# Weight parts kept in DRAM and an order from other durations, in the input projection of a decoder layer

## The chip, the cores and the metric

The kernel runs on one core of one Trainium2 chip. The metric is the device time of one execution in microseconds. The core's engines are TensorE (PE, matmuls; PEld is its weight loads), VectorE (DVE), ScalarE (ACT), GpSimd (POOL) and SyncE (SP), whose queue issues nearly all DMAs here.

## The reference

One layer of a hybrid decoder in float32, 2048 tokens of width 1024. Each half of the layer is normalised before and after. The first half projects the tokens once, splits the result into an mLSTM group and an attention group (MLA), and projects both back. The second half is an MLP.

```python
a   = rmsnorm(x, norm_pre_mix)
proj = a @ w_in                   # 1024 -> 1960 columns, 16 units of 128 in the kernel
qk_ml = silu(causal_conv(qk_ml, conv_w, conv_b))       # q, k of 4 mLSTM heads
h_ml = mlstm_chunkwise(q_ml, k_ml, v_ml, i_gate, f_gate)
h_ml = rmsnorm(h_ml) * sigmoid(o_ml)
q  = rmsnorm(c_q, q_norm) @ w_uq                       # c_q: 256 columns of proj
kv = rmsnorm(c_kv, kv_norm) @ w_ukv                    # c_kv: 128 columns
k_rope = apply_rope(k_r, cos, sin)
h_mla = causal_block_attention(q, k, v)                # 8 heads
x = x + rmsnorm(concat(h_ml, h_mla) @ w_out)
x = x + rmsnorm(square(relu(rmsnorm(x) @ w_up)) @ w_down)
```

## The kernel before, in words

Every float32 matmul is made of three matmuls in a faster 32-bit format (`mm3`, lines 198 to 200): each operand is split into a rounded part `h` (a cast) and the remainder `l` (a subtract), and h·h, h·l and l·h are summed. So every operand costs a cast and a subtract on other engines.

The input projection takes the tokens in four blocks of 512 (b = 0 to 3). Per block there are 16 units of 128 output columns; the units 13, 14, 15 are the latents of attention, 0 the gates and rotary keys, 1 to 4 the convolved q and k, 5 to 8 the values (whose four weights are used together), 9 to 12 the output gates. `ORDER` gives their sequence. For every block the weights of every unit are loaded anew from the input (`wu`, 512 KB), cast by ACT (line 376) and subtracted by DVE, or by Pool for the units in `WPOOL` (line 381). The raw tiles share four buffers (`awr`) with raw token tiles, the parts have four buffers each (`wh`, `wl`).

Behind a unit's matmuls come its own steps. For the latents (`latents_in`): multiply by the token scale (`norm` in block 0, `evac` later), square on ACT (line 537), sum over the partitions by TensorE with a column of ones (`sums_`, line 543, results in `ssp`), statistics, loads of the scale, gain and split. For the gates (`stabiliser`): transposes to token rows (`gates`), a polynomial of many small DVE steps (`g1` to `g3`), transposes back (`g4`, line 693, result `rp`), then scans. `chunk` is the mLSTM recurrence over 128 tokens, spread between the matmuls of values and gates.

Nothing of this order is left to chance. A planner (`Plan`) simulates all operations of the whole kernel with a duration for each (the number in `pl.op("DVE", 602, ...)`), buffer rings, and a key for priority; the sequence that it finds is pinned on TensorE, ACT, DVE and Pool, and DMA issues are emitted in it. On the chip each engine runs its instructions in that order and waits when one is not ready. Attention, the output projection and the MLP follow in the same plan; their first steps overlap with the last chunk.

Of the kernel before, what the change touches and what calls it, by code (L numbers as in the profile page):

```python
# [18 lines left out]
P = 128  # L19
# [29 lines left out]
QLO = 1  # L49
TLATE = 5.0  # L50
LEAD = 20.0
VLEAD = 3.0
# [4 lines left out]
XLEAD = 10.0  # L57
WLEAD = 18.0
SPLIT = 5.0
# [6 lines left out]
WPOOL = (1, 2, 3, 4)  # L66
LGAIN = 20.0
CPOOL = True
KPOOL = (0, 1, 2)
VPOS = (2, 2, 2, 4)  # L70
KROT = 50.0
XB = 4
FIN = (4, 6)
FK = 1.0
PINNED = ("PE", "Activation", "DVE", "Pool")
# [114 lines left out]
def trunk(ctx: ExitStack, tc: tile.TileContext, x, xT, pos, wu, uqw, ukw, uvw, wout, wup, wdn, cols, rows, consts, edge, out, dbg=None):  # L190
# [66 lines left out]
    for name, bufs in (  # L257
        ("awr", WR), ("wh", 4), ("wl", 4), ("mm", 2), ("pst", 1), ("cc", 1), ("cbc", 1), ("G", 1), ("raw", 2), ("cy", 2), ("cth", 2),
        ("rsbc", 2), ("tg", 1), ("R", 1), ("aS", 2), ("E", 2), ("iwbc", 1), ("qs", 1), ("num", 1), ("kv", 1), ("kw", 1), ("hn", HN), ("ho", HO),
        *((f"x{x}{k}", 2 if k < XDB else 1) for k in range(KD) for x in "hl"),  # L260
    ):
        pl.ring(name, bufs)
# [61 lines left out]
    def xsplit(b):  # L324
        def pair(j):
# [35 lines left out]

    def wsplit(b, u):
        t = {}
# [34 lines left out]
        t["free"] = [("wh", first[0][0]), ("wl", first[0][1])]  # L398
        return t

    unit_ops = []

    def unit(b, u):
        w = wsplit(b, u)
# [9 lines left out]
        for k in range(KD):  # L414
            last = pl.op(
                "PE", 648, lambda k=k: mm(k), [w["op"][k], *o_x[b, k]] + ([last] if k else []), kA(b, TIME[b][u]), take=() if k else ("mm",),
                free=w["free"] + x_holders[b, k],
            )
            if k == 0:
                t["head"] = last  # L420
            unit_ops.append(last)
# [3 lines left out]
    def statistics(nm, n, sums, o_sums, mul, add, key):  # L425
# [23 lines left out]
        o = pl.op("DVE", 75, ms, o_sums, key)  # L449
        t["op"] = o = pl.op("Pool", 300 + 165 * n, rs, [o, o_fill], key)  # L450
        if nm == "x0":
            return t
        h = pl.op("PE", 110, tr, [o, o_cst], key, take=("pst",))
        o = pl.op("DVE", 202, put, [h], key, free=[("pst", h)])
# [5 lines left out]
    def xstats(b):  # L460
# [27 lines left out]
        if b == 0:  # L488
            o_fill3.extend(pl.op("Pool", 1776, lambda i=i: fills3(i), ends if i else [x for k in range(4, KD) for x in o_x[0, k]], key=kA(0, 20)) for i in range(2))
# [19 lines left out]
        else:  # L509
            h = pl.op("PE", 860, spread, [t["op"], o_cst], key, take=("pst",))  # L510
            o_rsbc[b] = pl.op("Activation", 478, put, [h], key, take=("rsbc",), free=[("pst", h)])

    def latents_in(b):
# [4 lines left out]
        def one(i):  # L518
# [19 lines left out]

            def sums_():
                if i == 0:  # L540
# [5 lines left out]
            if b == 0:  # L546
                o = pl.op("Activation", 478, evac, [u["op"], *t.get("o", [])], key, take=take, free=[("mm", u["head"])])
                head = o
                o = pl.op("DVE", 602, norm, [o, o_rsbc[b]], key, free=[("rsbc", o_rsbc[b])])
            else:  # L550
                o = pl.op("DVE", 602, evac, [u["op"], o_rsbc[b], *t.get("o", [])], key, take=take, free=[("mm", u["head"]), ("rsbc", o_rsbc[b])])
# [3 lines left out]
            s = pl.op("Activation", 520, sq, [o], key, take=("cth",))  # L555
            o = pl.op("PE", 750, sums_, [s, o_fill, *sums], key, take=() if i else ("pst",), free=[("cth", s)])
# [6 lines left out]
        def total():  # L563
            ssc = e2.tile([P, 12], F32, tag="ssc", name=f"ssc{b}")
            vec.tensor_copy(ssc, t["p"][:, 0:12])
            ss8 = t["ss8"] = e2.tile([P, 8], F32, tag="ss8", name=f"ss8{b}")
            vec.tensor_tensor(ss8[:, 0:4], ssc[:, 0:4], ssc[:, 4:8], ALU.add)
            vec.tensor_scalar(ss8[:, 0:4], ss8[:, 0:4], QSCALE2 / 256, QSCALE2 * EPS, ALU.mult, ALU.add)
            vec.tensor_scalar(ss8[:, 4:8], ssc[:, 8:12], 1.0 / 128, EPS, ALU.mult, ALU.add)

        o = pl.op("DVE", 546, total, sums, key, free=[("pst", sums[0])])
# [13 lines left out]
        def split(i):  # L585
# [9 lines left out]
            g = pl.op("DVE", 663, lambda: gain(i), [l, o], late, free=[("cbc", l)])  # L595
            h = pl.op("Activation", 520, hi, [g], late, take=("cth",))
            d = pl.op("Pool" if CPOOL else "DVE", 1225 if CPOOL else 602, lo, [h], late)
# [11 lines left out]
    def rotate(b, t, G):  # L609
# [8 lines left out]

        eng, cost = (pool, ("Pool", 1225)) if b in KPOOL else (vec, ("DVE", 602))

# [15 lines left out]
        g = pl.op("SP", 500, load, o_rope, key, take=("tg",), kb=128)  # L636
# [3 lines left out]
        h = pl.op("Activation", 520, hi, [o], key)  # L640
# [6 lines left out]
    def stabiliser(b):  # L647
# [5 lines left out]
        def evac():  # L653
            t["Gr"] = e2.tile([P, TB], F32R, tag="G", name=f"G{b}", bufs=1)
# [131 lines left out]
    def conv(b, j):  # L786
# [35 lines left out]
        r = pl.op("Pool", 160, head, [o_fill, *halos.get((b - 1, j), [])], key, take=("raw",))  # L822
        e = pl.op("DVE", 602, evac, [r, u["op"], o_rsbc[b]], key, free=[("mm", u["head"]), ("rsbc", o_rsbc[b])])
        halos[b, j] = [pl.op("Pool", 160, tail, [e], key, free=[("raw", r)])]
        y = o = pl.op("Activation", 707, tap0, [e], key, take=("cy",), free=[("raw", r)])
        for i in range(1, 4):
            o = pl.op("DVE", 663, lambda i=i: tap(i), [o], key, free=[("raw", r)])
        h = pl.op("Activation", 520, tanh, [o], key, take=("cth",))
        war = [x for c in range(4) for x in o_chunk.get((b - 2, c), {}).get("qk", [])]
        o_qk[b, j] = [  # L830
            pl.op("DVE", 602, lambda i=i: put(i), [h, *war, *(o_fill3 if j < 2 else [])], key, free=[("cy", y), ("cth", h)])
# [3 lines left out]
    def values(b):  # L835

        ws = [wsplit(b, 5 + i) for i in range(4)]

        def one(c):
# [13 lines left out]
            for k in range(KD):  # L853
                last = pl.op(
                    "PE", 648, lambda k=k: mm(k), [ws[k // 2]["op"][0], *o_x[b, k]] + ([last] if k else []), kA(b, TIME[b][5 + c]),
# [6 lines left out]
            o_vx[b, c] = pl.op("Activation", 571, evac, [last, rs_x[b]["op"], *war], kA(b, TIME[b][5 + c] + 2), free=[("mm", head)])  # L862
# [4 lines left out]
    def gates(b, h):  # L867
# [9 lines left out]
        o = pl.op("DVE", 602, lambda: vec.tensor_tensor(g, u["p"], rsbc[b], ALU.mult), [u["op"], o_rsbc[b], *war], key, free=[("mm", u["head"]), ("rsbc", o_rsbc[b])])  # L877
        o = pl.op("Activation", 520, lambda: act.activation(g, g, AF.Tanh, scale=0.5), [o], key)
        o_gate[b, h] = pl.op("DVE", 396, gain, [o], key)

    def chunk(b, c):
# [121 lines left out]
        o = pl.op("Activation", 1172, exps, [e, o_sc_in[b]], key)  # L1003
        o = pl.op("Pool", 594, causal, [o], key)
        w = pl.op("DVE", 602, weigh, [o, s], key, free=[("aS", s)])
        q = pl.op("Pool", 1400, scale_q, [i, *qk], key, take=("qs",), free=[("iwbc", i)])
# [3 lines left out]
        k = pl.op("PE", 220, turn_k, [*qk, o_cst], key, take=("kv",))  # L1010
        kw = pl.op("DVE", 340, weigh_k, [k, o_sc_in[b]], key, take=("kw",), free=[("kv", k)])
        out["state"], out["v"], out["qk"] = [], [n], [s, q, k]
        for p in range(2):
            m = pl.op("PE", 430, lambda p=p: update(p), [kw, o_vx[b, c]], key, take=("kv",), free=[("kw", kw)])
            out["state"].append(pl.op("DVE", 528, lambda p=p: state(p), [m, n], key, free=[("kv", m)]))
            out["v"].append(m)
        a = pl.op("DVE", 273, norm1, [n], key)
        o = pl.op("Activation", 1106, norm2, [a], key)
        o = pl.op("DVE", 564, norm3, [o], key)
        o = pl.op("Pool", 958, norm4, [o, o_fill], key)  # L1020
        hn = pl.op("DVE", 680, norm5, [o], key, take=("hn",), free=[("num", n)])
        gs = [o_gate[b, i] for i in range(4)]
        h = pl.op("PE", 440, turn_h, [hn, *gs], key, take=("aS",), free=[("hn", hn)])
        g = pl.op("DVE", 602, gated, [h], key, take=("ho",), free=[("aS", h)])
# [3 lines left out]
    def rope_tables():  # L1028
# [5 lines left out]
        o2 = pl.op("DVE", 70, lambda: vec.tensor_scalar(off2, off, 2 * math.pi, None, ALU.mult), [o_rest], key)  # L1034
# [1514 lines left out]
```

## Time and profile before

| | |
|---|---|
| Median of 3 runs | 2485.22 us (2483.44 to 2487.77) |
| Profiled execution, its own time | 2481.76 us |
| Its span, first to last instruction | 2480.1 us |
| Input projection in the span | about 0 to 480 us |
| TensorE busy | 97% of the span |
| DMA moved | 378.14 MB, mean 152 GB/s |

The busy share of TensorE counts matmuls that overlap in its pipeline, so the distance from one matmul's start to the next says more than one's length. A released wait is named by the instruction whose end released it.

### The profile page before, as it was taken

What the parts mean: (1) busy time and instruction counts of PE and PEld (TensorE: products, weight loads), DVE (VectorE), ACT (ScalarE), POOL (GpSimd) and SP (SyncE); (2) the same over time, 40 slices, a digit from 0 to 9 for tenths busy, and PEclk for the clock granted to TensorE, in tenths of its full rate; (3) what the DMA queues carried; (4) which work ended last, traced back from release to release, by engine and by line L of the source; (5) the groups of instructions that cost most, each with busy time, mean ns of one, the idle gap of its engine ahead of it and who ended that gap; (6) DMA issues with size and microseconds to landing.
All of it is one profiled execution on the core that took longest, in us unless ns stands there. A gap on an engine that the chain in (4) does not pass through costs nothing.

```text
span 2480.1 us, 34020 instructions
## 1 busy us (share of the span) xinstructions
PE 2409.3 (97%) x11091; PEld 1940.9 (78%) x11091; DVE 1808.1 (73%) x3214; ACT 1349.9 (54%) x2625; POOL 863.6 (35%) x728
## 2 busy tenths in 40 slices
PE   8999999999999999999999999999999999999997
PEld 6778787767777777688888888888888888888875
DVE  5867667588888878745866678776676687776688
ACT  5535443367777777644666657665674343443343
POOL 3442424358898898532100000000000333332235
PEclk9999999999999999999999999999999999999998
DMA  6554544510000000476777799656574445445556
GB/s 222 150 164 144 171 152 134 146 49 15 17 21 12 13 15 11 146 230 217 263 215 212 236 283 275 201 167 186 170 238 151 153 129 178 132 143 157 188 165 226
DMA packets 308026, 378.14 MB, mean 152 GB/s; under 512 B 32028, under 2 KB 218408, under 8 KB 307656
## 3 DMA queue, kind: packets, MB, share of 16 engines
q1 hardware_dynamic: 304264, 368.58, 48.7%
q0 software_dynamic: 3584, 7.39, 1.1%
q8 instruction: 87, 1.43, 0.2%
q14 instruction: 91, 0.75, 0.1%
HBM read 251.93 MB, written 121.85 MB: 151 GB/s over the span
## 4 chain that ended last, share of the span: by engine, by line
PE 80%; DVE 9%; DMA 3%; POOL 3%; ACT 2%; issue 2%; SPq 1%; DVEq 0%; POOLq 0%; ACTq 0%
PE mm L198 2%; PE mm L199 2%; PE mm L200 2%; PE S L198 2%; PE m L1401 2%; PE o L1486 2%; PE op L198 2%; PE op L199 2%; PE S L199 2%; PE op L200 2%; PE S L200 2%; PE o L1489 2%; POOL t L1500 1%; DVE cy L809 1%; DVE y L2365 1%
## 5 line engine op out<-in xcount | busy, mean ns | idle before, releaser
L2381 POOL TENSOR_TENSOR y<-vd_0X,y 128x512 f32<-128x512 f32 x6 | 8.8, 1471 | 721.5 <-ACT vd_0X L2378 721.5
L1465 ACT ACTIVATE ph<-S 128x512 fp32r<-128x512 f32 (+1 forms) x320 | 170.5, 533 | 94.9 <-PE S L200 50.6
L1500 POOL TENSOR_TENSOR t<-t,ph 128x512 f32<-128x512 f32 (+1 forms) x192 | 211.3, 1101 | 19.9 <-ACT ph L1465 9.5
L2292 ACT CAST hh<-hr 128x512 fp32r<-128x512 f32 (+1 forms) x192 | 106.9, 567 | 159.0 <-DMA hr<-hd 38.1
L1473 DVE TENSOR_TENSOR pl<-S,ph 128x512 fp32r<-128x512 f32 (+3 forms) x272 | 157.4, 590 | 35.9 <-ACT S L1469 32.3
L198 PE MATMUL mm<-xh,wh 128*128 128x512 f32 x384 | 159.7, 416 | 9.4 <-ACT xh L342 8.2
L2297 DVE TENSOR_TENSOR hl<-hr,hh 128x512 fp32r<-128x512 f32 (+1 forms) x192 | 132.8, 701 | 35.1 <-ACT hh L2292 27.0
L1406 DVE TENSOR_REDUCE mp<-m 128x1 f32<-128x512 f32 x192 | 130.1, 684 | 31.4 <-PE m L1401 30.2
L199 PE MATMUL mm<-xl,wh 128*128 128x512 f32 x384 | 153.0, 398 | 0.0
L200 PE MATMUL mm<-xh,wl 128*128 128x512 f32 x384 | 152.9, 398 | 0.0
L1469 ACT ACTIVATE S<-S 128x512 f32<-128x512 f32 (+3 forms) x272 | 141.1, 519 | 0.1
L198 PE MATMUL S<-Qh,Kh 97*128 97x512 f32 (+1 forms) x320 | 121.4, 379 | 1.7 <-DVE pl L1473 1.4
L1486 PE MATMUL o<-ph,V 128*128 128x512 f32 (+1 forms) x320 | 119.4, 373 | 0.5 <-DVE ot L1559 0.5
L199 PE MATMUL S<-Ql,Kh 97*128 97x512 f32 (+1 forms) x320 | 117.8, 368 | 0.0
L1489 PE MATMUL o<-pl,V 128*65 128x512 f32 (+1 forms) x320 | 113.6, 363 | 4.2 <-DVE pl L1473 3.2
L200 PE MATMUL S<-Qh,Kl 97*128 97x512 f32 (+1 forms) x320 | 117.5, 367 | 0.0
L376 ACT CAST wh<-wr 128x1024 fp32r<-128x1024 f32 (+1 forms) x65 | 66.7, 1032 | 90.8 <-PE mm L199 62.4
L1401 PE MATMUL m<-Kh,Qh 96*128 96x512 f32 (+2 forms) x320 | 111.2, 383 | 1.7 <-DVE mp L1406 1.3
L2131 ACT ACTIVATE t<-t 128x512 f32<-128x512 f32 x96 | 60.6, 631 | 83.1 <-DVE t L2126 82.7
L198 PE MATMUL op<-wo,hh 128*128 128x512 f32 x256 | 101.1, 395 | 0.6 <-DVE x L1801 0.6
L199 PE MATMUL op<-wo,hh 128*128 128x512 f32 x256 | 99.9, 390 | 0.0
L200 PE MATMUL op<-wo,hl 128*128 128x512 f32 x256 | 99.8, 390 | 0.0
(6433 smaller groups left out, 7751.8 us busy)
## 6 DMA issues: line engine op xcount, KB each, us to landing
hr<-hd SPq DMA_DIRECT2D x92, 448.0 KB
hd<-t SPq DMA_DIRECT2D x128, 256.0 KB
wr<-in_wu_dram SPq DMA_DIRECT2D x63, 512.0 KB
hd<-ts SPq DMA_DIRECT2D x96, 256.0 KB
xt<-in_x_dram SPq DMA_DIRECT2D x28, 512.0 KB
xf<-xd SPq DMA_DIRECT2D x40, 256.0 KB
hr<-hT SPq DMA_DIRECT2D x64, 128.0 KB
x1d<-x SPq DMA_DIRECT2D x16, 512.0 KB
```

What stands on the lines that cost most here:

```text
L198: pe.matmul(o, ah, bh, start=start, stop=False)
L199: pe.matmul(o, ah, bl, start=False, stop=False)
L200: pe.matmul(o, al, bh, start=False, stop=stop)
L1401: pe.matmul(ps[:, :n], Qh[s][0:96, q0 : q0 + P], Kh[s][0:96, kb * TB : kb * TB + n], start=True, stop=True)
L1406: vec.tensor_reduce(mp["t"][:, j, kb : kb + 1], ps, axis=AX.X, op=ALU.max)
L1465: act.activation(t["h"][:, :w], t["S"][:, :w], AF.Exp)
L1469: act.activation(t["p"][:, :w], t["S"][:, :w], AF.Exp)
L1473: (pool if by_pool else vec).tensor_tensor(t["l"][:, :w], t["p"][:, :w], f32(t["h"][:, :w]), ALU.subtract)
L1486: pe.matmul(o0, v[:, 0:128], t["h"][:, :w], start=start, stop=stop)
L1489: pe.matmul(o1, v[:, 64:129], t["l"][:, :w], start=start, stop=stop)
L1500: pool.tensor_tensor(to, to, hv, ALU.add)
L2297: vec.tensor_tensor(t["l", m][:, :w], t["r", m][:, :w], f32(t["h", m][:, :w]), ALU.subtract)
```

## The change

For block 0 the weights are split as before. In block 1 they are split and both parts are also stored to a DRAM buffer `wparts`; in blocks 2 and 3 both parts are loaded from there, without cast and subtract. The squares of the first two latent tiles are added by Pool before TensorE sums them, so one of three groups of sums goes, and the DVE step that added the sums. Durations of the projection's operations in the plan are replaced, and so are lead times and keys; Pool subtracts units 1, 2, 9, 10 in place of 1 to 4; the rotation of blocks 1 and 2 goes from Pool to DVE; head 0's low parts go from DVE to Pool (`QLO`). Token splits of all blocks and weight splits are declared ahead of the rest, and a chunk's `turn_k` comes after the state update of the chunk before.

```diff
-QLO = 1
-TLATE = 5.0
+QLO = 0
+TLATE = 0.0
-VLEAD = 3.0
+VLEAD = 0.0
-XLEAD = 10.0
-WLEAD = 18.0
-SPLIT = 5.0
+XLEAD = 20.0
+WLEAD = 26.0
+SPLIT = 12.0
-WPOOL = (1, 2, 3, 4)
-LGAIN = 20.0
+WPOOL = (1, 2, 9, 10)
+LGAIN = 10.0
-KPOOL = (0, 1, 2)
+KPOOL = (0,)
-KROT = 50.0
+KROT = 90.0
+WSTORE = 5.0
+STB = (1,) * 16
+PIN = 684
...
+    wparts = dram.tile([16, 2, P, 1024], F32, tag="wparts", name="wparts")
+    def wload(b, u):
+        t = {}
+        def place(z):
+            t[z] = wp.tile([P, 1024], F32R, tag=f"w{z}", name=f"w{z}{b}_{u}")
+        def load(z):
+            dma(f32(t[z]), wparts[u, "hl".index(z)])
+        key = kA(b, TIME[b][u] - WLEAD)
+        o_turn[0] = g = pl.op("X", 0, lambda: [place(z) for z in "hl"], [o_turn[0]], key, take=("wh", "wl"))
+        a = [pl.op("SP", 500, lambda z=z: load(z), [g, *o_parts[u]], key + 0.01 * n, kb=512) for n, z in enumerate("hl")]
...
     def wsplit(b, u):
+        if b > STB[u]:
+            return wload(b, u)
...
+        for n, (z, o) in enumerate(zip("hl", first[-1])):
+            o_parts[u].append(pl.op("SP", 500, lambda n=n, z=z: dma(wparts[u, n], f32(t[z])), [o], kA(b, at + WSTORE), free=[(f"w{z}", first[0][n])], kb=512))
...
-                "PE", 648, lambda k=k: mm(k), ...
+                "PE", PIN, lambda k=k: mm(k), ...
...
+            def add():
+                pool.tensor_tensor(q["s"], t["q0"]["s"], q["s"], ALU.add)
...
-            o = pl.op("PE", 750, sums_, [s, o_fill, *sums], key, take=() if i else ("pst",), free=[("cth", s)])
+            if i == 0:
+                t["q0"], t["s0"] = q, s
+                return
+            if i == 1:
+                a = pl.op("Pool", 1320, add, [s, t["s0"]], key, free=[("cth", t["s0"])])
+            o = pl.op("PE", 970, sums_, [a if i == 1 else s, o_fill, *sums], key, take=() if i == 2 else ("pst",), free=[("cth", s)])
...
-            vec.tensor_tensor(ss8[:, 0:4], ssc[:, 0:4], ssc[:, 4:8], ALU.add)
...
-        o = pl.op("DVE", 391, g1, [h, o_rest], key, free=[("pst", h)])
-        o = pl.op("Activation", 106, g2, [o], key)
-        o = pl.op("DVE", 2986, g3, [o], key)
+        o = pl.op("DVE", 590, g1, [h, o_rest], key, free=[("pst", h)])
+        o = pl.op("Activation", 215, g2, [o], key)
+        o = pl.op("DVE", 3900, g3, [o], key)
...
-            o = pl.op("DVE", 663, lambda i=i: tap(i), [o], key, free=[("raw", r)])
+            o = pl.op("DVE", 720, lambda i=i: tap(i), [o], key, free=[("raw", r)])
...
-        k = pl.op("PE", 220, turn_k, [*qk, o_cst], key, take=("kv",))
+        k = pl.op("PE", 230, turn_k, [*qk, o_cst, *o_prev.get("v", [])[1:]], key, take=("kv",))
```

## Rows read from the trace of the kernel before

**Rows 1.** The page: busy us, share of the span and instructions by engine.

```profile
PE 2409.3 (97%) x11091; PEld 1940.9 (78%) x11091; DVE 1808.1 (73%) x3214; ACT 1349.9 (54%) x2625; POOL 863.6 (35%) x728
```

**Rows 2.** Windows, blocks 1 to 2: length, busy by engine, clock, DMA share, GB/s.

```profile
155.50:271.00 115.50, 112.33 (x533) 91.29 (x533) 77.66 (x159) 51.84 (x108) 42.24 (x39) 0.99 0.51 155
```

**Rows 3.** Waits of TensorE, 0 to 480 us: total, times, longest.

```profile
PE rp L693 <- DVE st L688: 6.3, 3, 2.5
PE kv L950 <- DVE C L955: 2.0, 2, 1.2
PE ssp L543 <- ACT sq L537: 1.5, 1, 1.5
...
PE tp L758 <- ACT R L747: 0.5, 1, 0.5
```

**Rows 4.** Timeline of TensorE around the polynomial's wait in block 1.

```profile
169.21 0.29 PE L693 MATMUL rp<-cst,st 128*16 128x128 f32 x1 [2.47 <-DVE st L688]
...
172.72 0.41 PE L200 MATMUL mm<-xh,wl 128*128 128x512 f32 x1
```

**Rows 5.** Windows of chosen stretches, with the columns of rows 2.

```profile
10.00:15.00 5.00, 5.00 (x18) 3.56 (x18) 5.00 (x8) 4.26 (x8) 0.00 (x0) 1.00 1.05 401
30.00:45.00 15.00, 13.51 (x55) 11.14 (x53) 6.81 (x9) 2.52 (x4) 8.50 (x4) 0.66 0.36 105
170.00:175.00 5.00, 5.00 (x18) 3.62 (x18) 3.61 (x16) 1.57 (x4) 2.00 (x2) 0.72 0.11 26
285.00:290.00 5.00, 5.00 (x18) 3.50 (x17) 3.82 (x17) 1.46 (x3) 2.06 (x2) 0.66 0.11 26
400.00:405.00 5.00, 4.93 (x24) 3.75 (x23) 4.76 (x16) 1.28 (x2) 0.69 (x1) 1.00 0.05 13
500.00:550.00 50.00, 44.78 (x235) 34.06 (x234) 44.52 (x94) 30.52 (x65) 25.41 (x23) 1.00 0.10 29
```

**Rows 6.** Timeline of TensorE around one group of sums in block 1.

```profile
142.60 0.95 PE L543 MATMUL ssp<-ones,sq 128*128 128x1 f32 x8
143.41 0.48 PE L198 MATMUL mm<-xh,wh 128*128 128x512 f32 x1
143.73 0.40 PE L199 MATMUL mm<-xl,wh 128*128 128x512 f32 x1
```

**Rows 7.** Groups by line, 0 to 480 us: busy us, mean ns; idle before, releaser.

```profile
L381 DVE TENSOR_TENSOR wl<-wr,wh 128x1024 fp32r<-128x1024 f32 x47 | 60.9, 1297 | 12.8 <-ACT wh L376 12.5
L809 DVE SCALAR_TENSOR_TENSOR cy<-raw,col,cy 128x512 f32<-128x512 f32 x48 | 41.0, 856 | 1.0
...
L530 DVE TENSOR_TENSOR cc<-mm,rsbc 128x512 f32<-128x512 f32 x9 | 6.2, 692 | 28.6 <-PE mm L200 28.6
...
L381 POOL TENSOR_TENSOR wl<-wr,wh 128x1024 fp32r<-128x1024 f32 x16 | 38.9, 2435 | 71.2 <-ACT wh L376 71.1
```

**Rows 8.** Timeline, block 3: the fourth value weight's cast and its first matmul.

```profile
440.41 1.05 ACT L376 CAST wh<-wr 128x1024 fp32r<-128x1024 f32 x1 [0.97 <-PE mm L199]
...
444.52 0.39 PE L198 MATMUL mv<-wh,xh 128*128 128x512 f32 x1
```

**Rows 9.** Timeline of SP's queue and ACT, block 2: loads of weights.

```profile
316.96 3.40 SPq L371 DMA_DIRECT2D wr<-in_wu_dram  x4
...
320.98 1.05 ACT L376 CAST wh<-wr 128x1024 fp32r<-128x1024 f32 x1 [2.24 <-DMA wr<-in_wu_dram]
```

**Rows 10.** Timeline of Pool and DVE, block 0: subtracts and norm multiplies.

```profile
26.62 7.93 POOL L381 TENSOR_TENSOR wl<-wr,wh 128x1024 fp32r<-128x1024 f32 x3
...
28.68 6.42 DVE L533 TENSOR_TENSOR cc<-cc,rsbc 128x512 f32<-128x512 f32 x3 [2.92 <-ACT rsbc L504]
```

**Rows 11.** Timeline of DVE and Pool at the start of attention.

```profile
490.05 0.68 DVE L1352 TENSOR_TENSOR Ql<-tq,Qh 96x512 fp32r<-96x512 f32 x1
...
491.70 2.27 POOL L1256 DMA_DIRECT2D c<-cd  x3
...
497.87 1.29 POOL L1473 TENSOR_TENSOR pl<-p,ph 128x512 fp32r<-128x512 f32 x1 [3.90 <-ACT p L1469]
```

More of the change, by code (lines that the diff above doesn't have):

```diff
@@ L415, in unit @@
             last = pl.op(
[L416 removed]
+                "PE", PIN, lambda k=k: mm(k), [w["op"][k], *o_x[b, k]] + ([last] if k else []), kA(b, TIME[b][u]), take=() if k else ("mm",),
                 free=w["free"] + x_holders[b, k],
@@ L593, in lo @@
                 (pool if CPOOL else vec).tensor_tensor(t["ccr"][:, i], t["cc"][:, i], f32(q["h"]), ALU.subtract)
-            g = pl.op("DVE", 663, lambda: gain(i), [l, o], late, free=[("cbc", l)])
-            h = pl.op("Activation", 520, hi, [g], late, take=("cth",))
-            d = pl.op("Pool" if CPOOL else "DVE", 1225 if CPOOL else 602, lo, [h], late)
+            g = pl.op("DVE", 710, lambda: gain(i), [l, o], late, free=[("cbc", l)])
+            h = pl.op("Activation", 570, hi, [g], late, take=("cth",))
+            d = pl.op("Pool" if CPOOL else "DVE", 1300 if CPOOL else 602, lo, [h], late)
             o_cds[i, b] = [
@@ L617, in load @@
             dma(t["tg"][64:128], trigd[:, b * TB : (b + 1) * TB])
-        eng, cost = (pool, ("Pool", 1225)) if b in KPOOL else (vec, ("DVE", 602))
+        eng, cost = (pool, ("Pool", 1350)) if b in KPOOL else (vec, ("DVE", 690))
         def d1():
@@ L835, in values @@
     def values(b):
-        ws = [wsplit(b, 5 + i) for i in range(4)]
+        ws = [W[b, 5 + i] for i in range(4)]
         def one(c):
@@ L1002, in chunk @@
         i = pl.op("SP", 1000, load_w, [o_sc_in[b, "wd"]], key, take=("iwbc",), kb=128)
[L1003 to L1006, printed above, removed]
+        o = pl.op("Activation", 1400, exps, [e, o_sc_in[b]], key)
+        o = pl.op("Pool", 640, causal, [o], key)
+        w = pl.op("DVE", 660, weigh, [o, s], key, free=[("aS", s)])
+        q = pl.op("Pool", 1560, scale_q, [i, *qk], key, take=("qs",), free=[("iwbc", i)])
         n = pl.op(
@@ L1033, in rope_tables @@
         key = kA(ROPE, 0)
-        o2 = pl.op("DVE", 70, lambda: vec.tensor_scalar(off2, off, 2 * math.pi, None, ALU.mult), [o_rest], key)
+        o2 = pl.op("DVE", 150, lambda: vec.tensor_scalar(off2, off, 2 * math.pi, None, ALU.mult), [o_rest], key)
         def half(q):
@@ L1093, in trunk @@
     o_rope = []
+    pl.group = "e2"
+    for b in range(NB):
+        xsplit(b)
+    rope_tables()
     for b in range(NB):
         pl.group = "e2"
-        xsplit(b)
-        if b == 0:
-            rope_tables()
         xstats(b)
```

137 lines of the change are left out of this document (76 added, 61 removed).

## The prediction, made before the result was known

> **What bounds the kernel now.** I read the page's busy shares first. TensorE is busy 97% of the span and no other engine passes 73% [rows 1], so outside TensorE's own work a change is worth only what it takes from TensorE's waits, or from TensorE itself. Of the 2480.1 us the diff rewrites the input projection, about the first 480 us. From the last sums of squares of block 1 to those of block 2 are 115.5 us, and TensorE is busy 112.3 of them, idle 3.2 [rows 2]. DVE is busy 67% of this stretch and Pool 37%: neither is full, but both run in a written order, and TensorE waits wherever an instruction stands earlier in that order than its data. Those waits are the next view, without the start [rows 3]: 6.3 us for the gate polynomial (`rp`, three times), 1.5 for the squares of block 0, and seven others from 2.0 (the state update) down to 0.5, together 7.4 us.
>
> The waits cost more than their length. In block 1 TensorE waits 2.47 us for `rp`; after it eight matmuls of 512 columns go by until 172.72, 3.5 us where eight at 0.23 are 1.8 [rows 4]; 1.6 us are lost. The row of that stretch shows a granted clock of 0.72 [rows 5], that is, more than half of it at the lower of the two levels (1.2 GHz). So this wait costs about 4. The like wait in block 2 is followed by a stretch with 0.66 of 5 us, 1.7 us lost [rows 5]. The third, 1.34 us in block 3, is followed by full clock [rows 5]. Sum for the polynomial: 6.3 + 1.6 + 1.7 = 9.6 us. In block 0, around the wait for the squares, the clock is 0.66 over 15 us: 5.1 us lost, with the wait 6.6 [rows 3, 5]. In all 9.6 + 6.6 + 7.4 = 23.6 us could be had by a perfect order. That is the ceiling for everything below except work that is removed.
>
> **Squares added first.** One group of sums (8 TensorE instructions) starts at 142.60, and the next matmul at 143.41: 0.81 us; that one then lasts 0.32 to its successor where 0.23 is usual, so 0.90 [rows 6]. One group of three goes in each of four blocks: 4 x 0.90 = 3.6 us less, and 32 fewer instructions. This is sure, since TensorE is the bound. In its place Pool adds two tiles; the nearest row, a Pool subtract of twice the columns at 2.435 us [rows 7], makes it an estimated 1.2 to 1.3. Its cover: the statistics feed loads that only attention reads. Without that cover it would be 1.3 us a block. DVE loses one small add a block, nothing on the path.
>
> **Weights kept in DRAM.** In blocks 2 and 3 the 32 casts on ACT (1.05 us each [rows 8]), and 24 of the subtracts on DVE (1.297) and 8 on Pool (2.435) go [rows 7]: 33 us of ACT, 31 of DVE, 19 of Pool over two blocks. None of these binds, so directly it is worth nothing; it takes DVE work out of the way of the conv taps and the gate polynomial, which stand before TensorE's waits. Rotation of blocks 1 and 2 moves from Pool to DVE, about 4 x 0.69 us each [rows 7], which takes back 5.5 of the 31.
>
> The price is DMA: block 1 writes 32 transfers of 512 KB, 16.8 MB, and blocks 2 and 3 each read 8.4 MB more. Block 1's stretch moves 155 GB/s at a share of 0.51 [rows 2], so 304 GB/s would fill it; 16.8 MB at that rate are 55 us, a share of 0.48 more, 0.99 in all. At the 401 GB/s of the first loads [rows 5] it is 42 us, 0.87 in all. It fits, barely by the slower rate. Lower bound 0; upper bound, if the rate falls short by a fifth, 0.19 x 115.5 = 22 us. I take 1, nearer the lower end, because weights are loaded ahead and TensorE waits for no DMA in this view [rows 3]. For blocks 2 and 3 the same sum gives 0.75 of the engines: no price from volume.
>
> Latency has one weak place. The four slots `wh`/`wl` hold the four value weights together, so the fourth gets its slot when the unit before the values ends. In block 3 the cast starts at 440.41, with the unit's last matmul; the first matmul of the fourth weight starts at 444.52 [rows 8]: 4.1 us from slot to use. A loaded weight has two transfers instead. Of four 512 KB loads that take 3.40 us to issue from 316.96, the first is used by the cast at 320.98 [rows 9]: 4.0 us, and 0.85 more for the second, 4.9. It is late by 0.8 us, twice 1.6. Lower bound 0 (in block 2, chunk work stands in between), upper bound both 3.3 us late with the clock's 1.5 behind them, 9.6. I take 1.6. The Trainium skill ("DMA: Bandwidth & Descriptors", Anatomy of one DMA) gives about 2.0 us fixed for a transfer, mostly the receipt, plus bytes at 436 GB/s. By that page both halves together take an estimated 4.4 us, and the sum would hold 0.6 in place of 1.6; its rule speaks against replacing a cast by a transfer at such a place, and the trace agrees on the order of size.
>
> **Order by other durations.** The polynomial's chain was planned at 391 + 106 + 2986 ns and now at 590 + 215 + 3900: 1.22 us later in every block. That covers 1.22 of the waits of 2.47, 2.47 and 1.34, and both falls of the clock, since 1.34 showed none: 3.7 + 3.3 = 7.0; with DVE freed in blocks 2 and 3 up to 9.6. I take 7. Lower bound 0, if the taps (planned 720, measured 856 [rows 7]) push the chain as far again. In block 0 the wait has another cause: three norm multiplies take 6.42 us, 2.1 each, while three weight subtracts run on Pool [rows 10]; the same kind of multiply takes 0.69 from PSUM [rows 7]. Two of these subtracts stay beside it, and the new add waits for the second square. I take half of 6.6, 3.3, with 0 and 6.6 as bounds. Of the other 7.4 us I take half, 3.7: the waits of blocks 2 and 3 go with the freed DVE, those at the rope tables need not.
>
> **Outside the projection.** Head 0's low parts (four of Q, one weight) move from DVE to Pool. DVE did the first in 0.68 us at 490.05; Pool issues DMAs one after another from then to 493.97, and a subtract of that size takes it 1.29 [rows 11]. If the low part queues behind them the first scores come up to 3.9 + 0.6 = 4.5 us later; if before, 0.6. From 500 to 550 DVE is the fuller one, 44.5 of 50 us against 25.4, so it can gain as well, at most TensorE's idle 5.2 there [rows 5]. I take a loss of 1, bounds 5 either way. The start (loads in another order) counts 0, cover: nothing; bounds 1 either way.
>
> **The sum.** 3.6 + 7 + 3.3 + 3.7 = 17.6 gained, 1 + 1.6 + 1 = 3.6 lost: 14 us. The profiled execution took 2481.8, so 2467.8; the median of the runs shown is 3.4 above it, so 2471.2, and I say 2471.
>
> **Rivals.** (1) Only removed work counts: the new order is as wrong elsewhere, waits are replaced by waits. For it: planned taps remain below measured ones. Against: three waits have one plain cause. 3.6 less up to 3: about 2483, no change. (2) Block 1 is bound by its DMAs: stores and loads share SP's one queue, a store that waits for a slow subtract holds the small loads behind it. For it: share 0.99 by the slower rate. Price up to 22, less the 14: 2493. It decides from the point where block 1 takes more than about 19 us longer than now. (3) All waits go: 3.6 + 23.6 less 2, 25 off 2485: 2460. (4) Head 0's start: the low parts behind Pool's issues and a longer slow clock, 5 us and 1.5 at the clock: 2478.
>
> **Numbers.** Forecast with its own range (2464 to 2477) 0.45; (3) 0.13; (4) 0.10; (1) 0.18; (2) 0.14. A difference under 0.2%, 5 us here, can't be told from no change. Faster by more: 0.45 + 0.13 + 0.08 of (4) = 0.66; the same: (1) and the rest of (4), 0.20; slower: (2), 0.14. The range leaves out part of (3) and part of (2): 2459 to 2491.
>
> **What would show it.** Right: 64 `ssp` instructions instead of 96, TensorE 11,059; `rp` waits under 1.5 us with full clock behind them; block paces near 112 us in blocks 2 and 3; 31 full-width casts of weights instead of 63; some 33 MB more moved. Wrong: TensorE waiting for weights from DRAM at the start of values by over 3 us; block 1 longer than 120 us with its DMA share near 1; a slower first 20 us of attention; or attention's own 500 us changed, which I counted as nothing.

## The result, and the profile after

The changed kernel takes 2464.97 us (median of 5 runs, 2461.73 to 2470.86) and the kernel before 2483.86 (5 runs, 2478.49 to 2487.77). The ratio is 0.9926, with a 95% interval of 0.9912 to 0.9939: 0.74% faster, 18.9 us. The profiled execution took 2464.97, with a span of 2463.3 where the one before had 2480.1. The kernel before was measured again beside each set of experiments: 2483.41 (e1 to e4), 2482.80 (e5 to e8) and 2481.67 (e9 to e12). Medians from different sets can so differ by about 2 us with no cause in the kernels; the ratios below are each taken against the set's own runs of the kernel before.

The page of the changed kernel, busy time by engine and the DMA lines. TensorE has the 32 instructions less that the prediction named; 33.6 MB more were moved (411.70 against 378.14).

```profile
PE 2399.6 (97%) x11059; PEld 1936.2 (79%) x11059; DVE 1777.7 (72%) x3189; ACT 1318.2 (54%) x2593; POOL 835.3 (34%) x721
...
DMA packets 317242, 411.70 MB, mean 167 GB/s; under 512 B 33052, under 2 KB 219432, under 8 KB 316872
```

TensorE's waits in the changed kernel from 0 to 480 us (total, times, longest). The first row is nearly all the start of the kernel (6.4 of it).

```profile
PE mm L204 <- ACT xh L348: 6.7, 2, 6.4
PE mm L204 <- DVE raw L842: 4.3, 3, 1.6
PE ht L1034 <- DVE hn L1027: 3.3, 1, 3.3
PE qq L204 <- DMA c<-cd: 2.0, 1, 2.0
PE tp L754 <- DVE rrc L481: 1.5, 1, 1.5
...
PE kv L995 <- DVE kw L988: 0.4, 1, 0.4
PE mv L205 <- DMA wl<-wparts: 0.4, 1, 0.4
PE kv L995 <- DVE C L1000: 0.4, 1, 0.4
```

Against [rows 3]: `rp` (6.3 us) is gone, `ssp` (1.5) is gone, the state update (`kv` for `C`, 2.0) is down to 0.4, with as much for `kw`. A new wait stands before the convolved units (`mm` for `raw`, 4.3 in all). `ht` and `qq` stand behind the projection's last matmul and count to attention's start. The only wait in this view for a weight from DRAM is 0.4 us.

Windows of the changed kernel, in the columns of [rows 2]: the stretch of block 0 that [rows 5] showed, and stretches inside blocks 1, 2 and 3.

```profile
30.00:45.00 15.00, 15.00 (x83) 12.37 (x81) 11.42 (x31) 5.40 (x8) 7.65 (x5) 1.00 0.39 129
124.00:237.00 113.00, 110.48 (x529) 90.53 (x528) 78.49 (x162) 51.81 (x108) 38.52 (x34) 1.00 0.84 307
241.00:350.00 109.00, 108.73 (x522) 89.20 (x521) 61.99 (x150) 35.20 (x90) 23.88 (x30) 1.00 0.66 235
350.00:455.00 105.00, 104.45 (x503) 85.44 (x502) 55.19 (x131) 26.19 (x70) 24.97 (x30) 1.00 0.61 204
```

The stretch from 30 to 45 has full clock (0.66 before [rows 5]), and so has each block; TensorE is idle 0.3 to 2.5 us in one. In blocks 2 and 3 DVE and Pool are much emptier: Pool is busy 23.88 of 109 us, where it was busy 42.24 of 115.5 in [rows 2]. Block 1 moves 307 GB/s at a share of 0.84, double the traffic, and TensorE waits for none of it.

The end of the projection, timeline of TensorE in the kernel before (its last projection matmul and the first of what follows):

```profile
474.23 0.40 PE L200 MATMUL mv<-wh,xl 128*128 128x512 f32 x1
474.46 0.60 PE L989 MATMUL ht<-cst,hn 128*128 128x128 f32 x4
```

and in the changed kernel:

```profile
453.21 0.39 PE L206 MATMUL mv<-wh,xl 128*128 128x512 f32 x1
453.44 1.02 PE L938 MATMUL S<-qbd,kT 128*128 128x256 f32 x4
```

So the projection ends 21.0 us earlier. The profiled spans differ by 16.8: behind the projection 4.2 us are given back. Each profiled execution is cut in this way in the table: the start of the first projection matmul (`first`); the distances from each block's first projection matmul to the next block's (`b0` to `b2`), and from block 3's first to its last (`b3`); the start of that last one (`last`); and the rest of the span.

Two columns need care. `first` scatters by some 2 us (6.4 for the changed kernel, 8.3 with nothing but attention's settings taken back, e8), but an early start is lost again within the first unit: the second unit starts at 16.2 and 16.4 in these two, and at 16.1 before. So `first` and `b0` are read together, as the start of block 1: 133.3 before, 125.1 changed. And `rest` is that of one execution, which can lie off its kernel's median: that of e3 took 5.6 less, that of e2 3.8 more, that of e8 3.2 more.

| kernel | median us | ratio to before (95%) | first | b0 | b1 | b2 | b3 | last | rest |
|---|---|---|---|---|---|---|---|---|---|
| before | 2483.86 | | 8.2 | 125.1 | 115.5 | 115.5 | 109.9 | 474.2 | 2005.9 |
| changed | 2464.97 | 0.9926 (0.9912 to 0.9939) | 6.4 | 118.7 | 112.0 | 109.5 | 106.6 | 453.2 | 2010.1 |
| e1_no_dram_parts | 2484.76 | 1.0001 (0.9991 to 1.0011) | 7.9 | 116.8 | 115.8 | 115.9 | 112.6 | 468.9 | 2010.7 |
| e2_durations_alone | 2490.13 | 1.003 (1.002 to 1.004) | 8.0 | 123.4 | 116.2 | 116.1 | 109.9 | 473.4 | 2018.8 |
| e3_dram_alone | 2477.89 | 0.997 (0.9959 to 0.9981) | 6.8 | 125.6 | 114.4 | 111.3 | 110.5 | 468.6 | 2002.0 |
| e4_sums_alone | 2477.97 | 0.9978 (0.9966 to 0.999) | 7.3 | 119.6 | 117.0 | 115.4 | 108.9 | 468.2 | 2008.4 |
| e5_no_pool_subtracts | 2480.29 | 0.9989 (0.9978 to 1.0) | 7.8 | 129.5 | 112.3 | 112.1 | 106.6 | 468.3 | 2012.0 |
| e6_old_gate_durations | 2468.43 | 0.9949 (0.9929 to 0.9968) | 8.1 | 115.7 | 112.4 | 110.5 | 105.7 | 452.5 | 2012.2 |
| e7_stores_only | 2481.9 | 0.9995 (0.9982 to 1.0007) | 8.1 | 117.6 | 112.8 | 117.0 | 113.3 | 468.9 | 2010.6 |
| e8_old_attention_settings | 2472.21 | 0.9961 (0.9947 to 0.9974) | 8.3 | 116.9 | 112.5 | 109.6 | 106.3 | 453.6 | 2020.1 |
| e9_pool_block0_no_parts | 2470.86 | 0.9954 (0.9937 to 0.997) | 8.3 | 116.6 | 114.6 | 112.1 | 106.8 | 458.4 | 2010.4 |
| e10_before_off_pool | 2478.38 | 0.9983 (0.9973 to 0.9994) | 7.8 | 125.7 | 114.4 | 112.4 | 107.3 | 467.7 | 2008.5 |
| e11_changed_pool_block0 | 2464.32 | 0.9926 (0.991 to 0.9943) | 6.5 | 118.4 | 110.3 | 112.2 | 106.5 | 453.8 | 2011.5 |
| e12_before_off_pool_sums | 2467.87 | 0.994 (0.9924 to 0.9956) | 8.6 | 118.7 | 113.3 | 111.4 | 106.3 | 458.3 | 2009.0 |

### The profile page after: what moved, and what is told of

It is laid out like the page before. It is cut to its first block, busy times and chain, and to the rows that moved or that the text cites. A ratio compares the mean times of both kernels' runs of the same rounds, so it can differ in the third digit from the quotient of the medians.

```text
span 2463.3 us, 34004 instructions
## 1 busy us (share of the span) xinstructions
PE 2399.6 (97%) x11059; PEld 1936.2 (79%) x11059; DVE 1777.7 (72%) x3189; ACT 1318.2 (54%) x2593; POOL 835.3 (34%) x721
## 2 busy tenths in 40 slices
DMA packets 317242, 411.70 MB, mean 167 GB/s; under 512 B 33052, under 2 KB 219432, under 8 KB 316872
## 3 DMA queue, kind: packets, MB, share of 16 engines
q8 instruction: 87, 1.43, 0.2%
## 4 chain that ended last, share of the span: by engine, by line
PE 82%; DVE 8%; POOL 3%; DMA 3%; issue 2%; ACT 1%; SPq 0%; DVEq 0%; POOLq 0%; ACTq 0%
PE mm L204 3%; PE mm L205 3%; PE mm L206 3%; PE S L204 2%; PE m L1447 2%; PE S L205 2%; PE S L206 2%; PE o L1532 2%; PE op L204 2%; PE op L205 2%; PE op L206 2%; PE o L1535 2%; POOL t L1546 2%; PE mv L205 1%; DVE y L2411 1%
## 5 line engine op out<-in xcount | busy, mean ns | idle before, releaser
L2338 ACT CAST hh<-hr 128x512 fp32r<-128x512 f32 (+1 forms) x192 | 106.8, 567 | 158.8 <-DMA hr<-hd 42.2
L2343 DVE TENSOR_TENSOR hl<-hr,hh 128x512 fp32r<-128x512 f32 (+1 forms) x192 | 133.3, 704 | 34.4 <-ACT hh L2338 26.2
L204 PEld LDWEIGHTS mm<-xh,wh 128*128 128x128 f32 x384 | 72.7, 189 | 28.8 <-ACT xh L348 7.4
```

The lines of the kernel that those rows point to most:

```text
L204: pe.matmul(o, ah, bh, start=start, stop=False)
L2343: vec.tensor_tensor(t["l", m][:, :w], t["r", m][:, :w], f32(t["h", m][:, :w]), ALU.subtract)
```

## The experiments

The prediction holds that the `rp` waits have one plain cause, planned durations that were too short, and that the weights in DRAM are directly worth nothing. The rival, raised by comparing the two traces: DVE's small instructions were stretched by Pool's, and whatever takes Pool's subtracts away from them takes the waits away.

**Each part alone.** Three edits of the kernel before take one part of the change each, and one edit of the changed kernel takes the DRAM parts out of it.

e1, changed kernel: the weights are split in every block, nothing is stored.

```diff
-STB = (1,) * 16
+STB = (9,) * 16
```

> The changed kernel, but weights are split anew in all four blocks and nothing is stored or loaded as parts. If the planned durations bring most of the gain, it stays: 2465 to 2470 us, at most 5 slower than the changed kernel. If the DRAM parts bring it, because DVE, ACT and Pool are freed in blocks 2 and 3, the 9.3 us gained there are gone and block 1 is no shorter than 113 us: 2474 or more.

It took 2484.76: all of the gain is gone, as the second expectation has it. Of TensorE's waits in it, 0 to 480 us, those for `bea` are new, three times up to 3.7 us.

```profile
PE tp L754 <- DVE bea L748: 11.0, 3, 3.7
...
PE tp L754 <- DVE bea L749: 2.3, 3, 0.8
```

`bea` is the end of the gates' scans. The scans in block 1 of e1, timeline of DVE and Pool:

```profile
164.95 2.38 POOL L411 TENSOR_TENSOR wl<-wr,wh 128x1024 fp32r<-128x1024 f32 x1
...
165.16 2.44 DVE L746 TENSOR_TENSOR_SCAN R<-zeros,R 16x128 f32<-16x128 f32 x1
```

A scan of 128 elements lasts 2.44 us, where it takes 0.41 in the changed kernel (rows below), and ends 0.27 after Pool's subtract. So `rp` did go, and a wait of the same chain, a few steps on, took its place.

e2, kernel before: the projection's durations of the change (some 70 lines like these) and the dependency of `turn_k`; nothing else.

```diff
-        o = pl.op("DVE", 2986, g3, [o], key)
+        o = pl.op("DVE", 3900, g3, [o], key)
...
-            o = pl.op("DVE", 663, lambda i=i: tap(i), [o], key, free=[("raw", r)])
+            o = pl.op("DVE", 720, lambda i=i: tap(i), [o], key, free=[("raw", r)])
...
-        k = pl.op("PE", 220, turn_k, [*qk, o_cst], key, take=("kv",))
+        k = pl.op("PE", 230, turn_k, [*qk, o_cst, *o_prev.get("v", [])[1:]], key, take=("kv",))
```

> The kernel before, with the new planned durations of the projection (and the order of turn_k that the plan needs with them), nothing else. If the durations bring most of the gain: about 2470 us (13 faster than before), and the waits of rp fall under 1.5 us. If the DRAM parts bring it: 2479 or more.

Measured: slower by 0.3%, 2490.13. The projection gains 0.8 us, not 7; the rest of the span is 12.9 longer in the profiled execution. TensorE's waits in it:

```profile
PE mm L199 <- DVE raw L798: 8.4, 5, 2.5
...
PE rp L694 <- DVE st L689: 4.3, 3, 1.8
```

The polynomial's wait shrinks by a third and another, 8.4 us, takes more than that.

e3, kernel before: parts stored in block 1 and loaded in blocks 2 and 3, with the same dependency and with the weight splits declared ahead; old durations, old sums.

```diff
+STB = (1,) * 16
...
+        if b > STB[u]:
+            return wload(b, u)
...
```

> The kernel before, with weight parts stored in block 1 and loaded in blocks 2 and 3 (and the order of turn_k), old durations and leads. If the durations bring the gain: 2479 to 2484 us, with the waits of rp as before. If the DRAM parts bring it: 2472 to 2476, with blocks 2 and 3 some 5 us shorter each.

Measured: 0.3% faster, 2477.89, between the two expectations. Block 2 gains 4.2 us, block 1, which stores, 1.1; block 3 is 0.6 longer. Its waits: `rp` stays in block 1 (2.5 us) and in block 2 (1.4), is gone in block 3, and the loads of values show.

```profile
PE rp L727 <- DVE st L722: 3.9, 2, 2.5
...
PE mv L201 <- DMA wl<-wparts: 0.8, 1, 0.8
PE mv L200 <- DMA wh<-wparts: 0.8, 1, 0.8
```

In block 2 Pool subtracts no weight any more, but still does the rotation, which in block 3 is DVE's. Timeline of DVE and Pool in block 2:

```profile
275.99 0.91 DVE L713 TENSOR_SCALAR sm<-sm 128x16 f32<-128x16 f32 x1 [0.28 <-ACT sm L709]
...
277.22 1.03 DVE L715 SCALAR_TENSOR_TENSOR sm<-sm 128x16 f32<-128x16 f32 x1
...
275.57 1.29 POOL L659 TENSOR_TENSOR tg<-G,tg 32x512 f32<-32x512 f32 x1
276.94 1.28 POOL L662 TENSOR_TENSOR G<-G,tg 32x512 f32<-32x512 f32 x1
```

In block 3 no Pool instruction is left beside the gate chain, and there `rp` is gone.

e4, kernel before: the squares of the first two latent tiles added on Pool.

```diff
...
+            if i == 0:
+                t["q0"], t["s0"] = q, s
+                return
+            if i == 1:
+                a = pl.op("Pool", 1320, add, [s, t["s0"]], key, free=[("cth", t["s0"])])
+            o = pl.op("PE", 750, sums_, [a if i == 1 else s, o_fill, *sums], key, take=() if i == 2 else ("pst",), free=[("cth", s)])
...
```

> The kernel before with only the squares added first, old durations. If the removed sums are worth what the trace says: 3.6 us, about 2480. If the wait for Pool's add takes it back, since TensorE's place for the sums is planned by old durations: 2483 to 2486, with waits of ssp over 1 us.

Measured: 2477.97, 0.2% faster, 5.4 us by the medians where 3.6 was expected. Block 1 starts 6.4 us earlier (126.9 against 133.3), so block 0 gives more than the whole. Of the 0.90 a block, blocks 1 to 3 show -1.5, 0.1 and 1.0; block 1 has new waits (`ptx` 1.4 us, `ht` 1.2). In block 0 the wait for the squares falls from 1.49 us to 0.93, and the window from 30 to 45 us has a clock of 0.89 in place of the 0.66 of [rows 5]:

```profile
30.00:45.00 15.00, 14.07 (x67) 10.96 (x66) 10.52 (x27) 3.68 (x7) 9.45 (x5) 0.89 0.45 141
```

**Pool beside DVE.** The kernel before already shows it. Timeline of DVE and Pool in block 1, ahead of the wait of [rows 4]:

```profile
162.00 2.40 POOL L381 TENSOR_TENSOR wl<-wr,wh 128x1024 fp32r<-128x1024 f32 x1
164.48 1.29 POOL L625 TENSOR_TENSOR tg<-G,tg 32x512 f32<-32x512 f32 x1
165.85 1.30 POOL L628 TENSOR_TENSOR G<-G,tg 32x512 f32<-32x512 f32 x1
...
162.42 2.02 DVE L679 TENSOR_SCALAR sm<-sm 128x16 f32<-128x16 f32 x1 [0.28 <-ACT sm L675]
164.47 0.25 DVE L680 RECIPROCAL sm<-sm 128x16 f32<-128x16 f32 x1
164.75 1.05 DVE L681 SCALAR_TENSOR_TENSOR sm<-sm 128x16 f32<-128x16 f32 x1
165.84 0.17 DVE L682 TENSOR_TENSOR sm<-sm 128x16 f32<-128x16 f32 x1
166.05 1.14 DVE L683 TENSOR_SCALAR sm<-sm 128x16 f32<-128x16 f32 x1
167.22 1.43 DVE L685 SCALAR_TENSOR_TENSOR sm<-sm 128x16 f32<-128x16 f32 x7
```

Three steps of 16 elements last 2.02, 1.05 and 1.14 us. Each starts while a Pool instruction runs and ends within 0.05 us of that one's end (164.44 and 164.40, 165.80 and 165.77, 167.19 and 167.15). Alone such a step takes 0.17, as L682 does, so 3.7 us are lost, more than the 2.47 that TensorE then waits. Block 2 shows the same three. The seven steps of L685 behind Pool's last one take 1.43 together, 0.2 each. The Trainium skill ("SBUF — State Buffer", Who interferes with whom) says that DVE and GpSimd share one pair of memory ports under an exclusive lock: an instruction of the one that needs the pair waits until the other's instruction has ended. These rows agree, to 0.05 us.

In block 3, whose wait is 1.34 us, the polynomial's steps are not stretched. There the rotation is on DVE and stands ahead of the polynomial, and its first step starts 0.01 us after a Pool subtract:

```profile
391.75 2.39 POOL L381 TENSOR_TENSOR wl<-wr,wh 128x1024 fp32r<-128x1024 f32 x1 [1.72 <-ACT wh L376]
...
391.76 2.92 DVE L622 TENSOR_TENSOR G<-G,tg 32x512 f32<-32x512 f32 x1
```

In e10, where Pool subtracts nothing in this block, the same step is

```profile
387.84 0.68 DVE L622 TENSOR_TENSOR G<-G,tg 32x512 f32<-32x512 f32 x1
```

So 2.2 us are lost here too, again more than TensorE then waits.

The same groups by line over 0 to 480 us (count, busy, mean ns) in the kernel before:

```profile
L679 DVE TENSOR_SCALAR sm<-sm 128x16 f32<-128x16 f32 x4 | 4.4, 1095 | 0.9 <-ACT sm L675 0.8
L681 DVE SCALAR_TENSOR_TENSOR sm<-sm 128x16 f32<-128x16 f32 x4 | 2.4, 612 | 0.1
```

and in the changed kernel, where they are L724 and L726 and the scan of e1's row is L746:

```profile
L746 DVE TENSOR_TENSOR_SCAN R<-zeros,R 16x128 f32<-16x128 f32 x4 | 1.6, 410 | 0.1
...
L724 DVE TENSOR_SCALAR sm<-sm 128x16 f32<-128x16 f32 x4 | 0.7, 175 | 0.4 <-ACT sm L720 0.3
L726 DVE SCALAR_TENSOR_TENSOR sm<-sm 128x16 f32<-128x16 f32 x4 | 0.7, 175 | 0.1
```

In e1 the mean of L746 is 1937 ns:

```profile
L746 DVE TENSOR_TENSOR_SCAN R<-zeros,R 16x128 f32<-16x128 f32 x4 | 7.7, 1937 | 0.1
```

The changed kernel still has Pool subtracts in block 1. One starts there 1.1 us after the scan's end, and the scan keeps its 0.41: what counts is whether the order puts the two side by side.

e5 is e1 without any weight subtract on Pool.

```diff
-WPOOL = (1, 2, 9, 10)
+WPOOL = ()
```

> As the run without DRAM parts (all weights split anew), but Pool subtracts no weights: DVE does all 16 units of each block. If those waits of 3.7 us for the scans in blocks 1 to 3 came from Pool's subtracts, which stretch DVE instructions beside them: the scans take 0.41 us again, the waits of tp for bea go, 2469 to 2477 us. If plain load on DVE caused them: 16 more subtracts of about 1.2 us make them longer, 2485 or more.

It took 2480.29, between the two expectations. The scans take 0.41 us again, the waits for `bea` fall from 13.3 us to 0.4, and blocks 1 to 3 take 112.3, 112.1 and 106.6 (115.8, 115.9 and 112.6 in e1), with more work on DVE and no weight in DRAM. Block 0 becomes 12.7 us longer than in e1, by a wait behind DVE, which now has all of its subtracts:

```profile
PE mm L204 <- DVE raw L842: 10.0, 4, 8.5
```

e9 therefore is e1 with Pool's subtracts in block 0 alone.

```diff
-        slow = u in WPOOL and not cut
+        slow = u in WPOOL and b == 0 and not cut
```

> The changed kernel without DRAM parts, Pool subtracting weights in block 0 only, DVE in blocks 1 to 3. If what the parts bring is that Pool no longer runs beside the scans of the gates: blocks 0 to 3 take 117, 112, 112, 107 us and the whole 2467 to 2471 us, within 5 of the changed kernel. If the parts are worth more (ACT, DVE): 2475 or more.

2470.86, inside the range of the first expectation (block 1 takes 114.6, where 112 was said): 13.9 of the 19.8 us that e1 lost come back by the medians (11.7 of 18.6 by the ratios), still without DRAM. The other 5.9 (7 by the ratios) are what the parts still add. In the profiled executions blocks 1 and 2 are 2.6 longer each in e9 (114.6 and 112.1 against 112.0 and 109.5). TensorE waits there for the value weights, which are cast by ACT and subtracted by DVE:

```profile
PE mv L204 <- ACT wh L406: 2.6, 2, 1.8
...
PE mv L205 <- DVE wl L411: 1.5, 2, 0.8
```

Of these 4.1 us the changed kernel has none in blocks 1 and 2, and 0.4 (for the load) in block 3. In block 2 the parts explain that; in block 1 the changed kernel splits its weights as well, only in another order.

e10 puts the same line into the kernel before, and the rotation of blocks 1 and 2 on DVE; durations stay the old ones.

```diff
-KPOOL = (0, 1, 2)
+KPOOL = (0,)
...
-        slow = u in WPOOL and not cut
+        slow = u in WPOOL and b == 0 and not cut
```

> The kernel before, old durations, no parts: only the weight subtracts of blocks 1 to 3 and the rotation of blocks 1 and 2 moved from Pool to DVE. If Pool's instructions stretch the gate polynomial on DVE (its steps of 0.17 us take 1 to 2 beside them) and so make the rp waits: those waits fall under 1 us each with full clock behind them, 2472 to 2477 us. If the old planned durations make them: they stay, and DVE's extra load makes 2483 to 2490.

TensorE has no wait for `rp` at all, and full clock where those waits stood (1.00 from 165 to 172, 280 to 287 and 394 to 400 us), with the polynomial planned as short as before. Its waits begin (behind the start) with

```profile
PE mm L198 <- DVE raw L797: 4.6, 4, 2.2
```

and L679 and L681 are back at 175 ns. Blocks 1 to 3 gain 6.8 us (1.1, 3.1 and 2.6). The gain in time is small: 2478.38, a ratio of 0.9983 (0.9973 to 0.9994), just outside the 2472 to 2477 expected. The wait for `raw`, 1.0 us before, takes some of it back.

e12 adds the sums of e4 to e10.

> The kernel before with the squares added first and those Pool instructions of blocks 1 to 3 moved to DVE; old durations, no parts. If the two gains add up: 5 for the sums and 8 for Pool, 2468 to 2473 us. If they are paid twice by the same waits: 2475 to 2478.

2467.87, 10.5 us under e10: block 1 starts 6.2 earlier (127.3 against 133.5), and blocks 1 to 3 are shorter by 1.1, 1.0 and 1.0. Against the runs of the kernel before in their own sets e4 gains 5.4, e10 3.3 and e12 13.8, more than the two together; why was not separated. It is within 3 us of the changed kernel (3.5 by the ratios) with none of its durations and nothing in DRAM.

**The other steps.** e6, changed kernel with the old durations of the gate chain and the rotation.

```diff
-        o = pl.op("DVE", 590, g1, [h, o_rest], key, free=[("pst", h)])
-        o = pl.op("Activation", 215, g2, [o], key)
-        o = pl.op("DVE", 3900, g3, [o], key)
+        o = pl.op("DVE", 391, g1, [h, o_rest], key, free=[("pst", h)])
+        o = pl.op("Activation", 106, g2, [o], key)
+        o = pl.op("DVE", 2986, g3, [o], key)
```

> The changed kernel with only the planned durations of the gate chain, from the transposes to the end of the scans, and of the rotation put back to the old ones. If these durations moved rp to where its data is ready: waits of rp come back, about 6 us and 3 of slow clock, 2472 to 2476. If the freed engines alone took the waits away: 2463 to 2468, rp waits under 1.5.

`rp` doesn't come back, and the projection ends at 452.5, as early as in the changed kernel. The median is 3.5 us higher (2468.43, 5.7 by the ratios); the rest of the span is 2.1 longer in the profiled executions.

e7, changed kernel that stores the parts in block 1, but splits anew in blocks 2 and 3.

```diff
-        if b > STB[u]:
-            return wload(b, u)
...
-        if b < STB[u]:
+        if b != STB[u]:
```

> The changed kernel with the stores of block 1, but blocks 2 and 3 split their weights anew and load no parts. If 16.8 MB of stores fill the DMA engines in block 1: block 1 longer than without stores (115.8 us) by 2 or more, 2487 or more. If they hide: block 1 at 115 to 116, 2481 to 2486 like the run without DRAM parts, and the gain of the parts is then all in what blocks 2 and 3 no longer do.

2481.9, as for stores that hide, but block 1 does not take the 115 to 116 said there: it takes 112.8 with the stores and 115.8 without (e1). No price shows; in the order with the stores no Pool subtract stands beside that block's scans, and its wait for `bea` (3.7 us in e1) is gone. Blocks 2 and 3 are long again (117.0, 113.3), with that wait.

e8, changed kernel with attention's old settings.

```diff
-QLO = 0
-TLATE = 0.0
+QLO = 1
+TLATE = 5.0
...
-VLEAD = 0.0
+VLEAD = 3.0
```

> The changed kernel with the three settings that only attention reads put back (head 0's low parts on DVE, the two leads). If Pool's queue holds the first scores up: the stretch behind the projection is 2 to 5 us shorter, 2460 to 2463. If its length follows the whole order by chance: anywhere within 5 us of 2465, and TensorE's first waits there unchanged.

2472.21, outside both expectations: the three new settings together are worth 7.2 us by the medians (8.7 by the ratios). The rest of the span is 10.0 longer without them in the profiled execution. They were not tried one by one.

e11, changed kernel with Pool's subtracts in block 0 alone (the line of e9), the version that the experiments pointed to.

> The changed kernel with DRAM parts, Pool subtracting weights in block 0 only, so that block 1 too is free of them. By the theory of Pool beside the scans: block 1 takes 109 to 111 us instead of 112 and the whole 2462 to 2464 us. If DVE's four more subtracts cost as much: 2465 to 2468.

2464.32, which can't be told from the changed kernel: block 1 gains 1.7 us (110.3, inside the 109 to 111 expected), block 2 loses 2.7, where TensorE waits 1.0 us for Pool's add of the squares.

## Why the prediction came out right, and which step failed

The time was 2464.97 for a predicted 2471, inside the forecast's own range, and faster as said. Of the sum, 15.0 us net were to come inside the projection and 1 was to be lost outside. Measured: 21.0, and 4.2 lost. The direction and size hold, but the reason given for the largest term doesn't. That the sum held is in part luck: the part that was priced at nothing did that step's work.

**Squares added first: right, but not as sure as said.** 32 instructions went, and e12 against e10 shows 1.1, 1.0 and 1.0 us in blocks 1 to 3, where 0.90 each was said. Alone in the kernel before (e4) the same edit shows -1.5, 0.1 and 1.0 there, since new waits took the place of the work removed. Pool's add costs no wait in the changed kernel, but 0.7 and 1.0 us in block 2 of e6 and e11.

**Block 0: mis-sized.** Said was 3.3, half of 6.6 us, under the new order. Block 1 starts 8.2 us earlier in the changed kernel (133.3 to 125.1); less 0.9 for the instructions that is 7.3, above the upper bound. It has no wait for the squares and full clock from 30 to 45 us. Most of it comes with the squares added first, which give 6.4 with the old durations (e4); the durations alone give 2.0 (e2, 131.3). The wait costs little in itself: in e4 it is still 0.93 us, but the stretch's clock is 0.89 instead of 0.66, which over 15 us is 3.5 us.

**Order by other durations: this step failed.** The prediction said that three waits "have one plain cause", and took 7 us for the longer planned chain. Longer durations alone give 0.8 us in the whole projection (e2); with the gate chain's taken back, no `rp` wait returns (e6); and with the old ones kept and Pool off these stretches, all of them go (e10). What the chain was late by is Pool's instructions beside it: 3.7 us of the polynomial in block 1 and as much in block 2, 2.2 us of the rotation ahead of it in block 3. So there was one cause, but another one than the planned durations. [rows 10] had shown the same in block 0, 6.42 us for three multiplies beside Pool's subtracts, and the prediction used it there, but it never looked for a Pool instruction beside the polynomial. So the rotation's move to DVE, which it booked as work added to DVE, is one of the edits that removed the wait: in block 2 of e3 Pool has the rotation but no subtract, and 1.4 us of the wait stay.

**Weights kept in DRAM: the price was about right, the worth was not.** The stores of block 1 cost nothing that can be seen (112.8 in e7, 110.3 in e11), where 1 was said and 22 was the bound; the rate at full share would be 307 / 0.84 = 365 GB/s, between the two that the bound used. The value weights' latency is a wait of 0.4 us in the changed kernel and 1.6 in e3; 1.6 was said. (The section of the Trainium skill that the prediction cites there describes transfers that GpSimd issues, while SP's queue issues these.) But pricing the parts at nothing failed: within the change they are worth 19.8 us (e1). They take the subtracts off DVE and Pool in blocks 2 and 3, and with them the stretching. e9 shows that 13.9 of it come back when Pool subtracts nothing after block 0, without DRAM.

**Other waits: replaced in part.** 3.7 of 7.4 us were to go. The state update's 2.0 fell to 0.8, `raw` rose from 1.0 to 4.3, and 1.5 for `rrc` came; in sum 7.4 us became 7.9, and nothing was won there. Rival (1), waits replaced by waits, was right for this and for e1 and e2 as a whole.

**Outside the projection: not covered.** Of the named signs of an error, attention's changed time is the one that came. The settings with Pool's low parts, priced as a loss of 1, are with the two leads a gain of 7.2 (e8). In the changed kernel the first low part is not behind Pool's DMA issues, which start at 468.99; timeline of Pool:

```profile
467.77 1.27 POOL L1398 TENSOR_TENSOR Ql<-tq,Qh 96x512 fp32r<-96x512 f32 x1 [5.16 <-ACT Qh L1395]
```

Against it stands a loss with the new durations: `rest` is 12.9 us longer in e2 and 14.2 in e8 than before, both with the old settings. Among the kernels with the old durations and the old settings (before, e3, e4, e10, e12) `rest` goes from 2002.0 to 2009.0; 2018.8 and 2020.1 are clear of that, the changed kernel's 2010.1 hardly. The start of attention shows part of what was lost in the changed kernel, in windows of 10 us behind the projection, first of the kernel before:

```profile
486.00:496.00 10.00, 7.90 (x26) 5.17 (x26) 5.21 (x15) 2.48 (x5) 5.01 (x11) 0.67 0.62 146
496.00:506.00 10.00, 9.08 (x50) 6.73 (x49) 7.93 (x18) 4.16 (x11) 1.29 (x1) 0.95 0.73 224
```

then of the changed one, 21 us earlier:

```profile
465.00:475.00 10.00, 6.51 (x24) 4.64 (x25) 4.73 (x13) 2.42 (x6) 6.22 (x13) 0.67 0.68 143
475.00:485.00 10.00, 9.57 (x38) 6.63 (x36) 5.39 (x13) 5.14 (x12) 3.29 (x3) 0.68 1.11 275
```

Both have a clock of 0.67 behind the waits at the end of the last chunk (`ht` 3.3 and `qq` 2.0 us in the changed kernel); before is back at 0.95 ten us later, the changed kernel is at 0.68, and that alone is 2.7 us. Which duration moves attention's order in this way was not separated and stays open. So does the changed kernel with every old duration: the runs only took back those of the gate chain and the rotation. The old lead times (`XLEAD`, `WLEAD`, `SPLIT`) were not tried in it either.

## What to carry to other kernels

When a chain of short instructions is late, lay the other engines' timelines beside it before correcting its planned durations: in these traces a step that ended together with another engine's instruction had been held by it, and no duration for the chain alone describes that. An engine that is 35% busy, like Pool here, can still set the pace by what it does to its neighbour, so the worth of removing "free" work from it is to be read at the chain that it stands beside. And take each part of a mixed change alone and out of the whole: here the durations alone lost time; the DRAM parts alone gave 5.5 us, and taken out of the whole they cost all of the gain.

## What the runs showed of the hardware

- A DVE step of 16 elements took 2.02 us beside a Pool subtract and 0.17 alone, and a scan of 128 elements 2.44 beside one and 0.41 alone. A reciprocal that began 0.01 us before a Pool instruction kept its 0.25. A multiply of 512 columns that began 0.01 us after one took 2.92, and 0.68 alone.
- The DVE multiplies of block 0 took 2.1 us each beside three Pool subtracts [rows 10], and 0.85 each in the changed kernel, where one subtract overlaps their first 0.8 us.
- Stores of 16.8 MB in one block beside the loads, 307 GB/s at a share of 0.84, left TensorE without a wait for a DMA in that block.
- The first matmul started at 6.4 us in one execution and at 8.3 in another of a kernel that differs in attention's settings alone; the second unit started at 16.2 and 16.4.
